# Two transformer blocks on one core: weight blocks at chosen SBUF offsets, and another order in two stages

## The chip, the cores and the metric

One Trainium2 chip, one of its cores. The metric is the device time of one launch in microseconds (us); the kernel before takes 2357.26 us, the median of 3 runs (2355.5 to 2357.8).

## The reference

Two different blocks run one after the other on `x` of 256 tokens by 1024 features, everything in float32; each block has two layers, l = 0 and l = 1.

```python
for l in range(2):                                   # first block
    h = rms(x, ln1[l]) * (1 + sc1) + sh1             # sc, sh, g from silu(c) @ w_mod[l]
    p = h @ w_in[l]                                  # 2756 columns
    # a: top-64 index attention, 4 heads;  b: stick breaking, 4 heads;  c: windowed attention, 8 heads
    x = x + g1 * (rms(concat(a, b, c), g_out[l]) @ w_o[l])
    h = rms(x, ln2[l]) * (1 + sc2) + sh2
    x = x + g2 * ((silu(h @ w_gate[l]) * (h @ w_up[l])) @ w_down[l])     # 2816 inner columns
for l in range(2):                                   # second block, with a context of 256 tokens
    h, hc = norms of x and ctx
    p, pc = h @ w_in_2[l], hc @ w_in_2[l]            # 13328 columns
    # A: mLSTM in both directions, 4 heads;  B: differential attention, 8 heads;  C: a 2-d Fourier mix
    x = x + gate * ((gA*(yA @ w_a_out) + gB*(yB @ w_b_out) + gC*(yC @ w_c_out)) @ w_out)
    ctx = the same for the context, in layer 0 only
```

## The kernel before

All float32 products that matter are made of three float32r matmuls: each operand is split into a part `hi` (rounded to float32r) and the rest `lo`, and hi·hi + hi·lo + lo·hi is summed in PSUM (`mm3`). The weights come from HBM in blocks of 128·kch rows by n columns (mostly 1024 by 256) into `raw` (2 buffers, issued on SP); ACT copies `raw` to `whi`, DVE (or POOL) subtracts into `wlo` (`split_half`, line 381, in two halves of a block). `whi` and `wlo` have two buffers each in the pool `w`, and `take` (line 417) hands a block to the stage that uses it.

A block is used in one of two ways. `dense_t` gives the transposed product: 128 columns of the weight block are the stationary operand of a matmul and h streams, 256 columns of it (one of x or the context) or 512 (both side by side). `dense_n` (called by `natural` and `natural2`) gives the natural product: h is stationary and 256 columns of weights stream. h is `h2`, hi and lo, 128 partitions by 8 chunks by 512 columns, in a pool on the right side of SBUF; the first block uses the 256 columns on its right half.

In time: conditioning and layer 0's mixing (to 219 us), layer 0's feed-forward `swiglu` (line 1172; gate and up 22 blocks, then down 12 blocks, whose moving operand is `ahi`, `alo` in the pool `pm`), layer 1's mixing (435 to 600) and feed-forward (to 807). Then the second block: in layer 0 heads A and pairs B (to 1100), Fourier branch C, gates and merges (1273 to 1713), output projection; in layer 1 the same (heads and pairs from 1795, C from 2001, gates and merges from 2112). In layer 0 x and the context run together, so `dense_t` streams 512 columns; layer 1 needs x alone in most products, 256 columns.

The order of the work is made when the program is built. A planner, the class `Clock`, keeps an estimated time of each engine. Dense blocks follow a fixed list, and the small steps between them (rope, statistics, scores, softmax, top-k, transposes) are items of a `Pipe`: at each tick the items whose inputs the planner holds for ready go one step on, in the order of their ranks. `prm` (line 210) gives the constants of a phase: 0 and 1 are the mixings of the two layers; 2 and 3, and 4 and 5, the two halves of the second block's layers 0 and 1. `RANK` orders the kinds of items of a mixing (sc cr ct cc ir it is sa ar at aa sb bo fc fa fb: `is` is index scores and top-k, `sa` the statistics and `at` the transposes of branch A, `ct` the transposes of branch C, `aa` its attends, `fb` the finish of A and B together). `SEQ` is the order of heads (a) and pairs (b); a third head or pair is begun when the first is drained. `BEHIND` holds items back when the planned DVE or ACT is more than so many us behind PE, `AHD` says how far ahead a raw load is issued, and `DY2` lists the small steps that may go to DVE or POOL, whichever is planned to be done earlier: `t` a copy of keys (`twice`), `s` the rsqrt chains of A and B, `o` those of `finish`.

Every engine has its own queue in that order, and waits only by semaphores; PE executes the matmuls as they were planned. SP's queue holds loads alone (`raw`, and `gw` for the small products `ps_g`). POOL's holds its small chains and the stores and loads of y.

Of the kernel before, what the change touches and what calls it, by code (L numbers as in the profile page):

```python
# [7 lines left out]
F32 = mybir.dt.float32  # L8
F32R = mybir.dt.float32r
# [12 lines left out]
KC = D // 128  # L22
WB = 256
# [5 lines left out]
QA, KA, VA, QI, KI, WI, QB, VB = 0, 256, 320, 384, 640, 704, 708, 1220  # L29

AQ, AK, AV, AG, AO, AZ, BQ, BK, BV, BZ, CU, CZ, MG = (0, 512, 1024, 2048, 2064, 3088, 4112, 5136, 6160, 7184, 8208,
                                                      9232, 10256)
# [169 lines left out]
        return self.clock.used.get(ring[-bufs], 0.0) if len(ring) >= bufs else 0.0  # L202


# [1 line left out]
DEF = dict(BEHIND=6.0, STARTS=2, SPL=2, AHD=1.0, SLACK=0.3, SPW=0.3, PB=0.5, DY2="x", TK=4, DYN=0, Y="", EVERY=2, SPOOL="",  # L206
           RANK="2 2 2 3 0 0 0 2 2 2 1 4 4 1 1 4", ENG="vvvpvpp", ORDER="IBCAV", SPN="0,0", ATT=3, SEQ="aababab", ADA="", ADS="")


def prm(ph):  # L210

    g = {'ADA_0': os.environ.get('ADA0','00 01'), 'ADS_0': os.environ.get('ADS0',''), 'ADA_1': os.environ.get('ADA1','10 11'), 'ADS_1': os.environ.get('ADS1',''), 'BEHIND_4': '1e9', 'BEHIND_5': '1e9', 'BEHIND_0': '8.0', 'BEHIND_1': '8.0', 'BEHIND_2': '1e9', 'BEHIND_3': '1e9', 'SPL_5': '2', 'SPL_4': '1', 'SPL_1': '3', 'SPL_0': '2', 'SPL_3': '2', 'SPL_2': '1', 'ATT_1': '2', 'ATT_0': '3', 'SLACK_2': '-1', 'SLACK_3': '0.3', 'SLACK_0': '0.3', 'SLACK_1': '0.3', 'SLACK_4': '-1', 'SLACK_5': '0.3', 'PB_0': '0.5', 'PB_1': '0.5', 'RANK_0': '0 2 2 3 0 4 0 4 4 1 1 4 4 0 0 3', 'RANK_1': '2 2 2 3 0 4 0 4 2 5 4 1 4 0 2 0', 'DYN_5': '1', 'DYN_4': '1', 'DYN_3': '1', 'DYN_2': '1', 'DYN_1': '1', 'DYN_0': '0', 'ORDER_0': 'IBCAV', 'ORDER_1': 'ICVAB', 'SPOOL_1': '1', 'SPOOL_0': 'x', 'Y_1': 'b', 'Y_0': 'ab', 'ENG_0': 'vpvppvv', 'ENG_1': 'vppvvpp', 'EVERY_1': '2', 'EVERY_0': '2', 'STARTS_5': '1', 'STARTS_4': '1', 'STARTS_3': '1', 'STARTS_2': '1', 'STARTS_1': '2', 'STARTS_0': '2', 'DY2_1': 'x', 'DY2_0': 'x', 'TK_1': '1', 'TK_0': '8', 'AHD_3': '4', 'AHD_2': '4', 'AHD_1': '2.0', 'AHD_0': '1.0', 'AHD_5': '4', 'AHD_4': '4', 'SPN_1': '0,0', 'SPN_0': '0,0'}.get
    p = types.SimpleNamespace(**{k: type(v)(g(f"{k}_{ph}", g(k, v))) for k, v in DEF.items()})
    p.ADA, p.ADS = [[tuple(int(i) for i in u) for u in s.split()] for s in (p.ADA, p.ADS)]
    return p
# [88 lines left out]
class Program:  # L304
# [21 lines left out]
    def phase(self, ph):  # L326
        p = self.p = prm(ph)
        if self.clock:
            self.clock.slow = ph in "01"
        self.pipe.starts, self.pipe.slack, self.pipe.most = p.STARTS, p.SLACK, p.BEHIND  # L330
# [40 lines left out]
    def fetch_g(self, j, now):  # L371
# [6 lines left out]
        self.gblk[j] = t  # L378
        return True

    def split_half(self, now=True):


        j = self.ns
        if j >= self.nd or (j >= 2 and j - 2 not in self.consumed):
            return False
        if not now and self.clock.ready([self.blk[j][0]]) > self.clock.t["pe"] + 1:
            return False
        raw = self.blk[j][0]
        kch, pieces = self.order[j]  # L390
        n = sum(p[4] for p in pieces)
        if self.half == 0:
            for i, nm in ((1, "whi"), (2, "wlo")):
                t = self.wp.tile([128, KC * WB], F32R, name=f"{nm}{j % 2}")
                self.blk[j][i] = t[:, :kch * n].rearrange("p (k c) -> p k c", k=kch)
        k0, k1 = ((0, (kch + 1) // 2), ((kch + 1) // 2, kch))[self.half]
        hi, lo = self.blk[j][1], self.blk[j][2]
        if k1 > k0:
            self.nc.scalar.copy(hi[:, k0:k1], raw[:, k0:k1])
            e = self.nc.gpsimd if str(self.half) in self.p.SPOOL and self.every else self.nc.vector  # L400
            e.tensor_tensor(lo[:, k0:k1], raw[:, k0:k1], hi[:, k0:k1].bitcast(F32), op=ALU.subtract)
        self.half += 1
        if self.half == 2:
            self.half = 0
            self.ns += 1
        return True
# [765 lines left out]
    def swiglu(self, l, h, begin):  # L1172
        nc, pm = self.nc, self.pm
        mod = self.mod[l]
        ahi = pm.tile([128, FC, L], F32R, name="ahi")
        alo = pm.tile([128, FC, L], F32R, name="alo")
        for f in range(FC):
            W = self.take([("w_gate", l, 0, 128 * f, 128), ("w_up", l, 0, 128 * f, 128)])
            ps = self.any_ps().rearrange("p (b t) -> p b t", b=2)
            for j in range(2):  # L1180
                self.dense_t(ps[:, j], W, 128 * j, h, 0, L)
            self.drop()
            th = pm.tile([128, L], F32, name="th", bufs=2)
            nc.scalar.activation(out=th, in_=ps[:, 0], func=AF.Tanh, scale=0.5)
            nc.vector.scalar_tensor_tensor(th, th, 1.0, ps[:, 0], op0=ALU.add, op1=ALU.mult)
            u = pm.tile([128, L], F32, name="mu", bufs=2)
            nc.vector.scalar_tensor_tensor(u, th, 0.5, ps[:, 1], op0=ALU.mult, op1=ALU.mult)
            self.split(u, ahi[:, f], alo[:, f])
            self.fill()
        norm = begin()  # L1190
        for b in range(4):
            pss = [self.any_ps()[:, :L] for j in range(2)]
            for k0 in range(0, FC, 8):
                kc = min(8, FC - k0)
                W = self.take([("w_down", l, 128 * k0, 256 * b, 256)], kc)
                for j in range(2):
                    self.dense_t(pss[j], W, 128 * j, (ahi, alo), 0, L, kch=kc, k0=k0, start=k0 == 0,
                                 stop=k0 + kc == FC)
                self.drop()
                self.fill()  # L1200
            for j in range(2):
                c = 2 * b + j
                nc.vector.scalar_tensor_tensor(self.x[:, c], pss[j], mod[:, 40 + c:41 + c], self.x[:, c],
                                               op0=ALU.mult, op1=ALU.add)
                self.norm_chunk(norm, self.x, c)
        return norm
# [642 lines left out]
    def run(self):  # L1849
# [51 lines left out]
        for l in range(DEPTH):  # L1901
            mod = self.mod[l]
            A = self.gain(mod[:, 8:16], self.ln[:, l, 0:8], f"A1_{l}") if l == 0 else None
            gate, scale = self.mod_gemv(l, 1), self.mod_gemv(l, 2)
            self.pending += [gate, scale] + [self.ada_gemv(*g) for g in prm(str(l)).ADA]
            if l:
                self.drain([ctx_ready])
# [21 lines left out]
            if upto == f"a{l}":  # L1929
                break  # L1930
            self.pending += [self.ada_gemv(*g) for g in prm(str(l)).ADS] + ([] if l else [self.mod_gemv(1, 0)])
            self.norm_rstd(n)
            if l == 0:
# [140 lines left out]
```

## Time and profile before

| what | value |
|---|---|
| median of 3 runs | 2357.26 us |
| lowest, highest | 2355.5, 2357.8 us |
| the profiled execution | 2364.57 us |
| its span, first to last instruction | 2362.8 us |
| its mean granted clock of TensorE | 0.969 |

The profile is of one execution. Busy times are of engines: PE is TensorE's matmuls, PEld its weight loads (beside PE), DVE VectorE, ACT ScalarE, POOL GpSimd. An end of a matmul is modelled, so the distance of starts tells more than the durations. The clock of TensorE has two levels, 2.4 GHz (1.00) and 1.2 GHz (0.50). Every instruction of this kernel goes through one helper, so all have line L170, and groups are told apart by the tiles: `ps_mm<-h,whi` streams h against stationary weights, `ps_mm<-whi,h` streams weights against stationary h.

### The profile page before, as it was taken

To read this page: it belongs to the slowest core of one execution; us is meant where nothing else is said; L and a number is where in the kernel's file an instruction comes from. 1 tells how busy PE (TensorE), PEld (TensorE's weight loads), DVE (VectorE), ACT (ScalarE), POOL (GpSimd) and SP (SyncE) were. 2 spreads that over 40 slices of the span, in tenths; PEclk is the share of its full clock that TensorE was granted. 3 is DMA by queue.
4 is the path that set the end of the run, shared out by engine and by line. 5 is a ranking of instruction groups with operands and counts; after the bars stand their busy time and mean duration, and the time that the engine had idled before them with its cause. 6 is when DMAs were issued, how large, how long until landed. Compare 5 with 4: busy or idle time off the path is not lost. (4 is left out here: it accounts for less than half of the span.)

```text
span 2362.8 us, 39015 instructions
## 1 busy us (share of the span) xinstructions
PE 2247.8 (95%) x15672; PEld 1974.9 (84%) x15672; DVE 1287.4 (54%) x2547; ACT 1032.1 (44%) x1994; POOL 371.7 (16%) x897
## 2 busy tenths in 40 slices
PE   7989999998899999997989999999999999989999
PEld 3756899876899988887878888888898897989999
DVE  3735556575556546666554424335364656655665
ACT  3543445445444444554543323223254445444543
POOL 3311001551000103122022000000020333220000
PEclk8978999998999999998999999999999999999999
DMA  9646985655686522122114434434343232337865
GB/s 331 230 159 220 288 252 181 212 188 196 197 243 187 173 89 72 56 82 72 61 65 139 128 91 113 119 94 114 96 131 90 81 99 74 106 114 201 211 172 170
DMA packets 395061, 348.52 MB, mean 148 GB/s; under 512 B 12768, under 2 KB 364384, under 8 KB 394368
## 3 DMA queue, kind: packets, MB, share of 16 engines
q1 hardware_dynamic: 386752, 321.29, 45.1%
q0 software_dynamic: 6688, 21.66, 2.9%
q10 hardware_dynamic: 1440, 3.08, 0.4%
q8 instruction: 123, 2.02, 0.4%
q14 instruction: 58, 0.48, 0.1%
HBM read 335.50 MB, written 10.49 MB: 146 GB/s over the span
## 5 line engine op out<-in xcount | busy, mean ns | idle before, releaser
L170 DVE TENSOR_TENSOR wlo<-raw,whi 128x1024 fp32r<-128x1024 f32 (+1 forms) x465 | 547.6, 1210 | 449.1 <-ACT whi L170 447.8
L170 ACT CAST whi<-raw 128x1024 fp32r<-128x1024 f32 (+3 forms) x476 | 471.5, 1031 | 216.1 <-PE ps_t L170 63.3
L170 PE MATMUL ps_mm<-whi,h 128*128 128x256 f32 x2752 | 533.9, 291 | 16.1 <-ACT whi L170 6.2
L170 PEld LDWEIGHTS ps_mm<-whi,h 128*128 128x128 f32 x2752 | 440.6, 194 | 48.7 <-issue 19.3
L170 PE MATMUL ps_mm<-wlo,h 128*128 128x256 f32 x1376 | 391.1, 284 | 7.5 <-DVE wlo L170 7.3
L170 PE MATMUL ps_mm<-h,whi 128*128 128x256 f32 (+2 forms) x1656 | 375.5, 321 | 1.9 <-DVE xT L170 1.8
L170 PEld LDWEIGHTS ps_mm<-h,whi 128*128 128x128 f32 (+1 forms) x1656 | 269.2, 187 | 46.9 <-issue 9.0
L170 PEld LDWEIGHTS ps_mm<-wlo,h 128*128 128x128 f32 x1376 | 266.8, 194 | 12.6 <-DVE wlo L170 8.4
L170 PE MATMUL ps_mm<-h,wlo 128*128 128x256 f32 (+2 forms) x828 | 263.0, 318 | 1.1 <-POOL wlo L170 1.1
L170 PE MATMUL ps_s<-h,whi 128*128 128x256 f32 (+1 forms) x1120 | 240.2, 310 | 0.0
L170 PE MATMUL ps_t<-h,whi 128*128 128x256 f32 (+1 forms) x1096 | 234.9, 310 | 2.1 <-ACT h L170 1.5
L170 PEld LDWEIGHTS ps_s<-h,whi 128*128 128x128 f32 x1120 | 181.3, 188 | 18.3 <-ACT th L170 5.6
L170 PEld LDWEIGHTS ps_t<-h,whi 128*128 128x128 f32 x1096 | 179.0, 190 | 19.8 <-ACT th L170 6.3
L170 PE MATMUL ps_s<-h,wlo 128*128 128x256 f32 (+1 forms) x560 | 173.4, 310 | 0.1
L170 PE MATMUL ps_t<-h,wlo 128*128 128x256 f32 (+1 forms) x548 | 169.5, 309 | 0.0
L170 PEld LDWEIGHTS ps_mm<-h,wlo 128*128 128x128 f32 (+1 forms) x828 | 155.1, 187 | 14.7 <-POOL wlo L170 1.3
L170 PE MATMUL ps_g<-gw,c 128*32 128x512 f32 (+1 forms) x640 | 100.8, 640 | 18.0 <-DMA gw<-in_w_mod_dram 8.7
L170 PEld LDWEIGHTS ps_s<-h,wlo 128*128 128x128 f32 x560 | 105.2, 188 | 7.0 <-DVE wlo L170 0.3
L170 PEld LDWEIGHTS ps_t<-h,wlo 128*128 128x128 f32 x548 | 104.2, 190 | 6.2 <-DVE wlo L170 0.2
L170 ACT ACTIVATE M<-ps_s,nmB,rsB 128x512 f32<-128x512 f32 (+1 forms) x96 | 67.0, 702 | 94.2 <-DVE nmB L170 94.2
L170 DVE SCALAR_TENSOR_TENSOR y<-th,y 128x512 f32<-128x512 f32 (+1 forms) x64 | 35.6, 556 | 81.2 <-ACT th L170 67.9
L170 POOL TENSOR_TENSOR sqa<-sqa,sq 128x256 f32<-128x256 f32 x30 | 22.1, 736 | 346.9 <-ACT sq L170 191.3
(406 smaller groups left out, 3726.8 us busy)
## 6 DMA issues: line engine op xcount, KB each, us to landing
raw<-in_w_in_dram SPq DMA_DIRECT2D x72, 1024.0 KB, 5.3
raw<-in_w_in_dram SPq DMA_DIRECT2D x100, 512.0 KB, 4.1
gw<-in_w_mod_dram SPq DMA_DIRECT2D x96, 512.0 KB, 5.3
gw<-in_w_ada_dram SPq DMA_DIRECT2D x64, 384.0 KB, 5.0
raw<-in_w_gate_dram SPq DMA_DIRECT2D x44, 512.0 KB, 4.1
raw<-in_w_up_dram SPq DMA_DIRECT2D x44, 512.0 KB, 5.6
raw<-in_w_down_dram SPq DMA_DIRECT2D x16, 1024.0 KB, 5.1
raw<-in_w_out_dram SPq DMA_DIRECT2D x12, 1024.0 KB, 5.2
```

The lines of the kernel that those rows point to most:

```text
L170: return real(*a, **k)
```

## The change

The blocks of weights get 128 more columns of room, and start at an offset of 0, 16 or 32 elements (0, 64 or 128 bytes), which `place` chooses from the first piece of the block: 0 for those that stream (`natural`, `natural2`, DFT), 16 for those that stand against 512 columns in the second block's layer 0 and for the gate columns AG, 32 for all others. A tile `apart`, which nothing writes or reads, stands behind `ahi` and `alo`; as the pool ends at a fixed address it moves them by 320 bytes in layer 0 and 416 in layer 1. The constants of `prm` change for the phases 0, 1 and 4.

```diff
 def prm(ph):
...
-     'RANK_1': '2 2 2 3 0 4 0 4 2 5 4 1 4 0 2 0'   'AHD_1': '2.0'   'DY2_0': 'x'
-     'BEHIND_4': '1e9'   'SLACK_4': '-1'   'AHD_4': '4'
+     'RANK_1': '2 2 0 3 0 4 5 0 2 1 4 1 4 0 2 2'   'AHD_1': '4.0'   'DY2_0': 't'
+     'BEHIND_4': '5.0'   'SLACK_4': '-1.0'   'AHD_4': '0.5'   'PB_4': '0.5'   'DY2_4': 'sto'   'SEQ_4': 'abaabab'
...
+    @staticmethod
+    def place(pieces):
+        name, l, r, c, w = pieces[0]
+        if name == "dft" or name == "w_in" and not QB <= c < VB:
+            return 0
+        if name == "w_in_2" and (AV <= c < AG or BQ <= c < BZ or CU <= c < CZ):
+            return 0
+        if name == "w_in_2" and (l == 0 or c in (AG,)):
+            return 16
+        return 32
...
-                t = self.wp.tile([128, KC * WB], F32R, name=f"{nm}{j % 2}")
-                self.blk[j][i] = t[:, :kch * n].rearrange("p (k c) -> p k c", k=kch)
+                t = self.wp.tile([128, KC * WB + 128], F32R, name=f"{nm}{j % 2}")
+                o = self.place(pieces)
+                self.blk[j][i] = t[:, o:o + kch * n].rearrange("p (k c) -> p k c", k=kch)
...
         ahi = pm.tile([128, FC, L], F32R, name="ahi")
         alo = pm.tile([128, FC, L], F32R, name="alo")
+        pm.tile([128, 104 if l else 80], F32, name="apart")
```

`SEQ_4` was the default aababab and `DY2_4` the default, which lets nothing choose. The diff also takes the environment variables out of `prm`, whose defaults stay.

## Rows read from the trace of the kernel before

**Rows 1.** The page's first part: busy us (share of the span) xinstructions

```profile
PE 2247.8 (95%) x15672; PEld 1974.9 (84%) x15672; DVE 1287.4 (54%) x2547; ACT 1032.1 (44%) x1994; POOL 371.7 (16%) x897
```

**Rows 2.** Windows: length, PE PEld DVE ACT POOL, PEclk, DMA share, GB/s

```profile
219.00:435.00 216.00, 213.51 (x1754) 196.51 (x1754) 125.73 (x199) 103.57 (x168) 14.58 (x16) 0.98 0.77 236
435.00:565.00 130.00, 115.61 (x816) 90.96 (x816) 79.89 (x221) 65.46 (x147) 65.58 (x104) 0.91 0.62 210
1400.00:1500.00 100.00, 100.00 (x439) 82.05 (x438) 43.94 (x51) 32.92 (x44) 4.29 (x8) 1.00 0.43 114
1795.00:2001.00 206.00, 203.40 (x1465) 181.54 (x1464) 123.73 (x280) 102.19 (x215) 59.33 (x182) 0.99 0.28 87
2112.00:2363.00 251.00, 247.26 (x2115) 246.67 (x2114) 153.92 (x223) 113.54 (x172) 13.96 (x27) 1.00 0.69 188
```

**Rows 3.** Windows of dense stretches, weights stationary, 256 columns

```profile
54.60:59.80 5.20, 5.20 (x47) 5.20 (x45) 2.36 (x2) 1.27 (x2) 4.28 (x14) 1.00 1.03 367
195.40:198.10 2.70, 2.70 (x26) 2.57 (x25) 0.48 (x1) 0.01 (x1) 0.00 (x0) 1.00 0.62 187
708.00:745.00 37.00, 37.00 (x329) 37.00 (x328) 25.09 (x35) 18.48 (x27) 0.00 (x0) 1.00 0.70 199
746.00:807.00 61.00, 61.00 (x518) 61.00 (x517) 30.04 (x35) 27.17 (x37) 4.86 (x7) 1.00 0.62 194
2160.00:2290.00 130.00, 130.00 (x1106) 130.00 (x1105) 81.20 (x116) 60.85 (x92) 4.29 (x8) 1.00 0.71 190
2303.00:2353.00 50.00, 50.00 (x444) 50.00 (x443) 34.46 (x50) 22.93 (x33) 0.00 (x0) 1.00 0.68 195
```

**Rows 4.** Windows of dense stretches, weights moving

```profile
48.40:53.20 4.80, 4.80 (x44) 4.75 (x42) 3.40 (x5) 2.30 (x4) 4.80 (x9) 1.00 1.00 358
2058.00:2062.80 4.80, 4.80 (x43) 4.80 (x42) 3.14 (x4) 2.58 (x4) 4.06 (x10) 1.00 0.00 0
2080.60:2083.00 2.40, 2.40 (x23) 2.40 (x22) 1.01 (x3) 1.32 (x3) 0.19 (x1) 1.00 0.00 0
```

**Rows 5.** Timeline of PE after a start, weights moving: start us, us, instruction

```profile
2027.20 0.28 PE L170 MATMUL ps_mm<-wlo,h 128*128 128x256 f32 x1
...
2027.56 0.28 PE L170 MATMUL ps_mm<-wlo,h 128*128 128x256 f32 x1
...
2028.02 0.39 PE L170 MATMUL ps_mm<-whi,h 128*128 128x256 f32 x2
...
2028.36 0.39 PE L170 MATMUL ps_mm<-whi,h 128*128 128x256 f32 x2
```

**Rows 6.** Timeline of PE: 512 columns, twice, and the DFT's 256

```profile
837.62 0.63 PE L170 MATMUL ps_mm<-h,whi 128*16 128x512 f32 x2
...
841.80 0.39 PE L170 MATMUL ps_mm<-h,whi 128*16 128x512 f32 x1
...
1272.64 0.88 PE L170 MATMUL ps_t<-pq,dft 128*128 128x256 f32 x6
1273.35 0.39 PE L170 MATMUL ps_mm<-h,whi 128*128 128x512 f32 x1
...
1804.34 0.63 PE L170 MATMUL ps_mm<-h,whi 128*128 128x512 f32 x2
...
1808.54 0.63 PE L170 MATMUL ps_mm<-h,whi 128*128 128x512 f32 x2
```

**Rows 7.** Groups by line of DVE, 434 to 606: xcount | busy, mean

```profile
L170 DVE MATCH_REPLACE8 idx_w<-m,idx_w 128x256 f32<-128x256 f32 (+1 forms) x16 | 5.3, 340 | 0.0
...
L170 DVE MAX8 m<-idx_w 128x8 f32<-128x256 f32 (+1 forms) x16 | 4.9, 346 | 0.0
```

**Rows 8.** Timeline of DVE: the mask's last write and its first reader

```profile
522.07 0.32 DVE L170 TENSOR_TENSOR madd<-madd,masks 128x128 f32<-128x128 f32 x1
...
544.47 0.48 DVE L170 CUSTOM_DVE_ANT_0 S<-ps_s,madd,rs 128x256 f32<-128x256 f32 x1
```

**Rows 9.** PE's waits, 435 to 606: us in total, times, longest

```profile
PE ps_t L170 <- ACT S L170: 3.8, 2, 2.5
```

More of the change, by code (lines that the diff above doesn't have):

```diff
@@ L202, in free @@
         return self.clock.used.get(ring[-bufs], 0.0) if len(ring) >= bufs else 0.0
-import os, types
+import types
 DEF = dict(BEHIND=6.0, STARTS=2, SPL=2, AHD=1.0, SLACK=0.3, SPW=0.3, PB=0.5, DY2="x", TK=4, DYN=0, Y="", EVERY=2, SPOOL="",
@@ L210, in prm @@
 def prm(ph):
-    g = {'ADA_0': os.environ.get('ADA0','00 01'), 'ADS_0': os.environ.get('ADS0',''), 'ADA_1': os.environ.get('ADA1','10 11'), 'ADS_1': os.environ.get('ADS1',''), 'BEHIND_4': '1e9', 'BEHIND_5': '1e9', 'BEHIND_0': '8.0', 'BEHIND_1': '8.0', 'BEHIND_2': '1e9', 'BEHIND_3': '1e9', 'SPL_5': '2', 'SPL_4': '1', 'SPL_1': '3', 'SPL_0': '2', 'SPL_3': '2', 'SPL_2': '1', 'ATT_1': '2', 'ATT_0': '3', 'SLACK_2': '-1', 'SLACK_3': '0.3', 'SLACK_0': '0.3', 'SLACK_1': '0.3', 'SLACK_4': '-1', 'SLACK_5': '0.3', 'PB_0': '0.5', 'PB_1': '0.5', 'RANK_0': '0 2 2 3 0 4 0 4 4 1 1 4 4 0 0 3', 'RANK_1': '2 2 2 3 0 4 0 4 2 5 4 1 4 0 2 0', 'DYN_5': '1', 'DYN_4': '1', 'DYN_3': '1', 'DYN_2': '1', 'DYN_1': '1', 'DYN_0': '0', 'ORDER_0': 'IBCAV', 'ORDER_1': 'ICVAB', 'SPOOL_1': '1', 'SPOOL_0': 'x', 'Y_1': 'b', 'Y_0': 'ab', 'ENG_0': 'vpvppvv', 'ENG_1': 'vppvvpp', 'EVERY_1': '2', 'EVERY_0': '2', 'STARTS_5': '1', 'STARTS_4': '1', 'STARTS_3': '1', 'STARTS_2': '1', 'STARTS_1': '2', 'STARTS_0': '2', 'DY2_1': 'x', 'DY2_0': 'x', 'TK_1': '1', 'TK_0': '8', 'AHD_3': '4', 'AHD_2': '4', 'AHD_1': '2.0', 'AHD_0': '1.0', 'AHD_5': '4', 'AHD_4': '4', 'SPN_1': '0,0', 'SPN_0': '0,0'}.get
+    g = {'ADA_0': '00 01', 'ADS_0': '', 'ADA_1': '10 11', 'ADS_1': '', 'BEHIND_4': '5.0', 'BEHIND_5': '1e9', 'BEHIND_0': '8.0', 'BEHIND_1': '8.0', 'BEHIND_2': '1e9', 'BEHIND_3': '1e9', 'SPL_5': '2', 'SPL_4': '1', 'SPL_1': '3', 'SPL_0': '2', 'SPL_3': '2', 'SPL_2': '1', 'ATT_1': '2', 'ATT_0': '3', 'SLACK_2': '-1', 'SLACK_3': '0.3', 'SLACK_0': '0.3', 'SLACK_1': '0.3', 'SLACK_4': '-1.0', 'SLACK_5': '0.3', 'PB_0': '0.5', 'PB_1': '0.5', 'RANK_0': '0 2 2 3 0 4 0 4 4 1 1 4 4 0 0 3', 'RANK_1': '2 2 0 3 0 4 5 0 2 1 4 1 4 0 2 2', 'DYN_5': '1', 'DYN_4': '1', 'DYN_3': '1', 'DYN_2': '1', 'DYN_1': '1', 'DYN_0': '0', 'ORDER_0': 'IBCAV', 'ORDER_1': 'ICVAB', 'SPOOL_1': '1', 'SPOOL_0': 'x', 'Y_1': 'b', 'Y_0': 'ab', 'ENG_0': 'vpvppvv', 'ENG_1': 'vppvvpp', 'EVERY_1': '2', 'EVERY_0': '2', 'STARTS_5': '1', 'STARTS_4': '1', 'STARTS_3': '1', 'STARTS_2': '1', 'STARTS_1': '2', 'STARTS_0': '2', 'DY2_1': 'x', 'DY2_0': 't', 'TK_1': '1', 'TK_0': '8', 'AHD_3': '4', 'AHD_2': '4', 'AHD_1': '4.0', 'AHD_0': '1.0', 'AHD_5': '4', 'AHD_4': '0.5', 'SPN_1': '0,0', 'SPN_0': '0,0', 'PB_4': '0.5', 'DY2_4': 'sto', 'SEQ_4': 'abaabab'}.get
     p = types.SimpleNamespace(**{k: type(v)(g(f"{k}_{ph}", g(k, v))) for k, v in DEF.items()})
```

## The prediction

> **What bounds the kernel now.** I read the page first: TensorE (PE) is busy for 95% of the span, every other engine for 54% or less [rows 1]. Then the busy time stage by stage, for the question where PE waits at all. In the feed-forward of layer 0 (219 to 435 us) it is idle for 2.5 us of 216, in the gates and merges of layer 0's second block not at all (1400 to 1500), in layer 1's merges and output for 3.7 of 251 [rows 2]. There the end is set by how closely matmuls follow each other. DMA reaches a share of 0.77 in the fullest of these stages and VectorE (DVE) 126 of 216 us, so a somewhat faster PE has both behind it. Only the mixing of layer 1 (435 to 565 us) shows slack: PE idle 14.4 us of 130, mean granted clock 0.91, that is 23 us at the 1.2 GHz level [rows 2].
>
> So the number to read is the spacing of matmuls in dense stretches. A window's count holds about 2.4 matmuls that began before it (a record is 0.28 us long), so the spacing is the window over count less 2.4. With the weight block as stationary operand and 256 columns streaming, the spacing is 37.0/326.6 = 113.3 ns in the stretch at 708 us and 50.0/441.6 = 113.2 ns at 2303, but 130/1103.6 = 117.8 ns at 2160, with the same tiles at the same addresses [rows 3]. Nothing waits in either. A stretch thus runs at one of two paces, quick (113.3) or slow (117.8), and keeps it until a gap. Of these stretches 6, with 1,036 matmuls, are quick (first and last in [rows 3], at 195.4 and 2303) and 56 slow (first and last at 54.6 and 2160). The down projection, whose moving operand ahi stands at other addresses than h, runs at 61/515.6 = 118.3 ns in layer 1, never quick [rows 3].
>
> With the operands exchanged (weights stream, h is stationary) it is the other way round: 81 of 133 stretches are quick (first and last at 48.4 and 2080.6), 52 slow (one at 2058, 4.8/40.6 = 118.2) [rows 4]. What differs is the start address of the stationary operand less that of the moving one, modulo 256 bytes: in the built program h2 stands at 224 and the weight blocks at 160, so it is 192 with the weights stationary and 64 with the weights moving; for ahi it is 128 (layer 0) and 32 (layer 1). Of 46 stretches at 64 that begin 215 to 230 ns after the matmul before, 34 settle quick; of 44 such at 192, 3. One that settles begins at 2027: three matmuls take 0.36 us first (2027.20 to 2027.56) and 0.34 a few later (2028.02 to 2028.36) [rows 5].
>
> **The places.** The change moves no instruction here: ACT and DVE write the same elements at another offset, which I cost at nothing (PE never waits in [rows 2] at 1400, with ACT and DVE busy 33 and 44 us of 100). Place 32 moves the stationary blocks by 128 bytes, and the pads move ahi to 224, so that every 256-column matmul with stationary weights gets the difference 64. From the loops there are 6,336 of these: 2,112 in gate and up, 1,056 in down, 1,152 in layer 1's merges, 768 in its gates, 576 in the two output projections of the second block, 384 in w_o, 192 in q and k of the first block's stick heads, 96 in layer 1's aqT. Today they cost 5,300 x 4.5 ns + 1,056 x 0.5 ns (ahi, both layers at layer 1's pace) = 24.4 us more than at the quick pace. If three in four are quick, as 34 of 46 suggest, 1,584 x 4.5 = 7.1 us stay: **17.3 us gained**. Ends: all quick, 24.4; none quick, a loss of 4.1 (the quick stretches of today are two long ones, 908 matmuls, and four short).
>
> The 4,128 matmuls with moving weights keep place 0 and their difference of 64: nothing.
>
> The 512-column matmuls of layer 0's second block go to place 16, difference 0; 2,256 with layer 1's 24 for the gates and its 96 of akT, which get place 32 but are priced with them. They run at 100/(439-1.7) = 228.7 ns [rows 2] (a record of 0.39 us spans 1.7 of them). No stretch of the trace has 512 columns at a steady 0. Nearest rows: a stretch of akT in layer 1 at 233.3 ns (18 matmuls from 1804.34 to 1808.54); the gate columns, whose difference walks through 192, 0, 64 and 128 as k advances, at 4.18/18 = 232.2 ns; and 256 columns at 0 in the DFT, 0.71/6 = 118 ns, not quick [rows 6]. That speaks for a loss, up to 2,256 x 4.6 = 10.4 us. On the other side, the quick 256-column pace is 6.6 ns over 256 columns at 2.4 GHz (106.7 ns); the same excess over 512 columns would be 220, a gain of 19.6 us. I take the middle of these ends, 226.6 ns, since no row is nearer to one than to the other: **4.7 us gained**.
>
> A rule speaks against all of this, in sentences the sum does without. The Trainium skill's page "SBUF — State Buffer", section "SBUF: two separate sides", says that TensorE's reads never wait for anyone, and its page "TensorE: Matmul & The Clock Gate", section "Step-by-step: what each phase is for", that loading the next weights takes no SBUF bandwidth from the running matmul. By these an address cannot matter and the places are worth 0 instead of 22 us; the trace sides against them in the 118.3 of ahi and the unequal shares of quick stretches, and with them in that one address shows both paces.
>
> **The order.** Layer 1's mixing: the index scores and the top-k drop from first to last rank, the statistics and transposes of branch A rise. The top-k is 16 MAX8 and 16 MATCH_REPLACE8, 10.2 us of DVE [rows 7]; the mask made from it is done at 522 and its first reader, an attend of A, comes at 544 [rows 8], so 22 us of attends of C and of the stick heads hide the move. If that cover goes, attend A waits, behind it on PE the w_o blocks: up to +10 (the 10.2 us laid bare). What it could free is PE's wait for S, 3.8 us [rows 9], and some of the half-clock time, 23 us which cost 11.7: up to -9. I take **2 us gained**. AHD_1 issues raw loads earlier on SP, where only loads (raw and gw) stand; PE shows no wait for DMA there: nothing. DY2_0 lets two small copies of layer 0 go to DVE: nothing, since PE has other blocks to run beside them; were one laid bare it is some tenths of a us.
>
> Layer 1's second block (1795 to 2001): PE is idle 2.6 us of 206 at clock 0.99 [rows 2], so another order of heads and pairs can gain 3 us at most. The moved steps' DMAs: raw loads on SP in the order of use, and the y stores on POOL, each of which waits for DVE at the queue's head with the rsqrt chains behind it; 's' takes those chains away from there to DVE, busy 124 of 206 us. BEHIND_4 makes the plan hold items back when DVE or ACT runs 5 us behind; PE would then wait at the drains, at most the 5 us. I take nothing, -3 to +5.
>
> **Sum.** 17.3 + 4.7 + 2 = 24 us. The profiled execution took 2364.57 us (span 2362.8 and 1.8 around it): 2340.6 for it. The median of the runs is 7.3 us lower, 2357.26, which gives **2333.3**.
>
> **Rivals.** (B) Both groups settle: all 256-column ones quick and the 512-column ones at 220: 24.4 + 19.6 + 2 = 46 us, 2311. For: the pace once quick is kept through 444 matmuls [rows 3]; against: the DFT at difference 0 [rows 6]. (C) The places do nothing: only how a stretch starts decides. Then 2355 with the order's 2 us, 2357 without; this is also what the skill's rule gives. For: one address, two paces; against: ahi. (D) Slower: place 16 puts the 440 us of 512-column matmuls on 233.3 ns, +10.4 us, while the long 256-column stretches draw the slow pace, +4.1: 2357.3 + 14.5 - 2 = 2370. With a share p quick the 256-column gain is 28.5p - 4.1, so D decides below p = 0.44.
>
> **How the numbers follow.** Forecast 0.46 (own range 2320 to 2346), B 0.22, C 0.15, D 0.17. A measurement of this kernel tells 0.2% (4.7 us) from no change. Faster: forecast, B and 0.04 of C, 0.72; same 0.11; slower 0.17. The range runs from below B to the top of C, 2306 to 2360, and leaves out D and a little of B.
>
> **What would show it.** Right: in the changed trace the windows over the two feed-forwards and layer 1's merges hold about 444 matmuls per 50 us where they are dense, instead of 427; down is no longer at 118.3; a window of 100 us in the merges of layer 0 holds 443 or more instead of 439; the stretches with moving weights are as mixed as now. Wrong: some 430 there (D), the same mix of paces at every difference (C), or a mixing of layer 1 whose PE idle time rises over 20 us. The forecast fails if the share of quick stretches at 64 does not carry over from moving to stationary weights: that is its weakest step.

## The result, and the profile after

The changed kernel takes 2335.07 us, the median of 6 runs (2324.4 to 2344.74), beside 2357.53 for the kernel before: a ratio of 0.9897, 95% interval 0.9866 to 0.9928, so 17 to 32 us less. The forecast was 2333.3, its range 2306 to 2360. The profiled execution is the slowest of the six: 2344.74 us, span 2343.0.

First the page's first part, of the kernel after, as in [rows 1]:

```profile
PE 2228.7 (95%) x15672; PEld 1961.0 (84%) x15672; DVE 1311.5 (56%) x2637; ACT 1031.5 (44%) x1995; POOL 343.5 (15%) x779
```

PE has the same 15,672 instructions and 19.1 us less of busy time; the span fell by 19.8 us. Time went out of matmuls, not out of waits. Where, is read from windows cut at the same matmul in both kernels (first matmul of a stage to the first of the next). The columns are those of [rows 2]. Before; in order gate and up, down, the whole of layer 1's mixing, gate and up, down, the 512-column gates and merges, then from there to layer 1's branch C, and to the end:

```profile
243.15:369.79 126.64, 126.64 (x1064) 116.17 (x1056) 72.81 (x103) 54.45 (x82) 0.00 (x0) 1.00 0.86 261
369.79:434.05 64.26, 64.26 (x545) 64.26 (x544) 38.08 (x61) 37.55 (x64) 11.46 (x12) 1.00 0.57 181
434.05:622.42 188.37, 165.45 (x1198) 135.06 (x1197) 114.99 (x301) 92.12 (x197) 73.55 (x112) 0.91 0.58 192
622.42:745.25 122.83, 122.83 (x1058) 114.48 (x1057) 72.86 (x104) 54.58 (x82) 0.00 (x0) 1.00 0.78 230
745.25:807.73 62.48, 62.48 (x531) 62.48 (x529) 30.56 (x35) 27.80 (x39) 4.86 (x7) 1.00 0.60 189
1273.35:1712.83 439.48, 439.48 (x1923) 360.58 (x1922) 176.83 (x205) 129.18 (x165) 14.65 (x28) 1.00 0.41 112
1712.83:2063.28 350.45, 337.41 (x2505) 308.62 (x2504) 209.99 (x449) 172.74 (x353) 92.09 (x262) 0.98 0.31 95
2063.28:2359.38 296.10, 288.95 (x2422) 283.12 (x2420) 180.44 (x281) 136.89 (x231) 26.06 (x67) 0.99 0.64 176
```

The same stages after:

```profile
235.81:358.16 122.35, 122.35 (x1059) 112.38 (x1057) 72.84 (x103) 54.73 (x82) 0.00 (x0) 1.00 0.87 265
358.16:420.89 62.73, 62.73 (x544) 62.73 (x543) 38.08 (x61) 37.49 (x63) 11.46 (x12) 1.00 0.58 185
420.89:610.34 189.45, 166.14 (x1198) 131.87 (x1197) 113.27 (x300) 92.07 (x199) 74.39 (x112) 0.91 0.60 198
610.34:730.73 120.39, 120.39 (x1058) 114.38 (x1057) 75.07 (x106) 54.88 (x82) 0.00 (x0) 1.00 0.77 224
730.73:790.57 59.84, 59.84 (x530) 59.84 (x529) 30.58 (x35) 27.60 (x39) 4.87 (x7) 1.00 0.62 197
1257.32:1692.56 435.24, 435.24 (x1923) 360.37 (x1922) 177.07 (x205) 128.97 (x165) 14.67 (x28) 1.00 0.41 113
1692.56:2044.66 352.10, 335.48 (x2509) 306.66 (x2508) 224.43 (x532) 172.84 (x353) 62.49 (x163) 0.98 0.31 95
2044.66:2339.56 294.90, 290.32 (x2418) 284.31 (x2416) 181.31 (x289) 136.19 (x231) 21.42 (x48) 0.98 0.63 176
```

PE is busy through all of the five dense stages in both kernels, at clock 1.00, and each is shorter: 4.3 + 1.5 + 2.4 + 2.6 + 4.2 = 15.1 of the 19.8 us. The mixing of layer 1 is 1.1 us longer, the stages between the fifth and the sixth row together 1.1 us longer, the last two stages together within half a us. Layer 0's mixing, ahead of these rows, was 7.4 us shorter, which the experiments take back: it scatters.

Then the pace, in windows of dense stretches after (as [rows 3], and 100 us of the same stage as the window of [rows 2] at 1400; the first row is from layer 0's down):

```profile
395.00:415.00 20.00, 20.00 (x172) 20.00 (x171) 15.22 (x25) 11.88 (x20) 1.47 (x2) 1.00 0.57 180
678.00:728.00 50.00, 50.00 (x443) 50.00 (x442) 33.09 (x46) 25.24 (x38) 0.00 (x0) 1.00 0.70 196
735.00:785.00 50.00, 50.00 (x443) 50.00 (x443) 25.13 (x27) 22.85 (x32) 4.87 (x7) 1.00 0.63 199
1300.00:1400.00 100.00, 100.00 (x443) 82.81 (x442) 29.12 (x31) 25.09 (x30) 0.54 (x1) 1.00 0.40 104
2130.00:2260.00 130.00, 130.00 (x1106) 130.00 (x1105) 78.30 (x107) 61.23 (x90) 4.29 (x8) 1.00 0.73 196
2282.00:2332.00 50.00, 50.00 (x443) 50.00 (x442) 35.08 (x50) 24.32 (x35) 0.00 (x0) 1.00 0.68 200
```

Gate and up, layer 1's down, and the end of layer 1's merges are quick, 50/(443 - 2.4) = 113.5 ns; layer 1's down was never quick before. Layer 0's down is quick for its first 230 matmuls only; the other 298 of its 528 run at the slow pace, 20/(172 - 2.4) = 117.9 ns. The 512-column window holds 443 instead of 439: 226.6 ns. But the long stretch of layer 1's merges (1,343 matmuls) is as slow as before, with 1106 in 130 us. Counted over the stretches, 45 of the 58 with stationary weights are quick, and with them 4,056 of 6,195 matmuls.

### The profile page after: what moved, and what is told of

Same layout as the page of the kernel before. It is cut to its first block, busy times and chain, and to the rows that moved or that the text cites. A ratio compares the mean times of both kernels' runs of the same rounds, so it can differ in the third digit from the quotient of the medians.

```text
span 2343.0 us, 38997 instructions
## 1 busy us (share of the span) xinstructions
PE 2228.7 (95%) x15672; PEld 1961.0 (84%) x15672; DVE 1311.5 (56%) x2637; ACT 1031.5 (44%) x1995; POOL 343.5 (15%) x779
```

## Experiments

All ratios are to the kernel before in runs of the same chip, with 95% intervals. Paces are mean distances of starts within a dense stretch; stage lengths are taken as in the windows above. The difference of two start addresses is that of the prediction, and an address is on the 32-byte grid when it is a multiple of 32. Of the one long line of constants in `prm` the diffs show only those that change.

**1. The places alone, and the order alone.** Run e1 is the changed kernel with the constants of before (places and pads alone); run e2 is the kernel before with the changed constants. The edit of e1, that of e2 is its reverse:

```diff
-    'RANK_1': '2 2 0 3 0 4 5 0 2 1 4 1 4 0 2 2'   'AHD_1': '4.0'   'DY2_0': 't'
-    'BEHIND_4': '5.0'   'SLACK_4': '-1.0'   'AHD_4': '0.5'   'PB_4': '0.5'   'DY2_4': 'sto'   'SEQ_4': 'abaabab'
+    'RANK_1': '2 2 2 3 0 4 0 4 2 5 4 1 4 0 2 0'   'AHD_1': '2.0'   'DY2_0': 'x'
+    'BEHIND_4': '1e9'   'SLACK_4': '-1'   'AHD_4': '4'
```

> The places and the pads alone, with the constants of the kernel before, so that the order of the instructions stays the old one. Theory P (the places bring the gain, by the pace of matmuls): 2335 to 2341 us, 256 columns with stationary weights at a mean of some 115.0 ns, 512 columns at 226.7, and single runs that differ by up to 10 us, as the pace is drawn anew at each start. Theory O (the other order brings a good part, as the first mixing is 7.4 us shorter in the changed kernel's profile): 2343 to 2348. Theory N (places do nothing): 2357.

> The constants of the changed kernel alone, weights and ahi at the old places. Theory P: 2355 to 2360 us, since the stages that the order touches add up to little. Theory O: 2346 to 2352 (7.4 us from layer 0's mixing, given back in part by layer 1's). In both the paces stay as before: 229.0 ns for 512 columns, 117.8 for nearly all stretches with 256.

Places: 2341.77 us, 0.9928 (0.9910 to 0.9945), 13 to 21 us less. Order: 2357.13, 0.9988 (0.9977 to 0.9999), 0.2 to 5.4 us less. The gates and merges of layer 0's second block in the two, places first; with them layer 1's merges with the places, and layer 0's gate and up with the order alone:

```profile
1254.88:1690.12 435.24, 435.24 (x1922) 360.37 (x1921) 176.91 (x205) 129.01 (x165) 14.65 (x28) 1.00 0.40 113
2120.00:2250.00 130.00, 130.00 (x1150) 130.00 (x1149) 79.70 (x109) 62.68 (x91) 4.29 (x8) 1.00 0.75 205
```

```profile
236.70:362.93 126.23, 126.23 (x1058) 116.17 (x1057) 72.82 (x103) 54.76 (x82) 0.00 (x0) 1.00 0.84 257
1264.88:1704.34 439.46, 439.46 (x1922) 360.60 (x1921) 177.14 (x205) 129.25 (x165) 14.65 (x28) 1.00 0.40 112
```

With the places the 512-column stage is 435.24 us to the hundredth, with the old ones 439.5, whatever the order. And the long stretch of layer 1's merges came out quick here, 1150 matmuls in 130 us, by the same addresses as above. So the places bring nearly all, theory P, though the time lies just above its 2335 to 2341; the order is a small gain. Theory O falls: layer 0's mixing takes 231.3 us with the old order too (230.3 and 231.0 in two other runs, e4 and e11), so the 237.5 of the profile before was a long draw.

**2. What of an address counts.** Run e3 gives every weight block of the changed kernel another offset, two blocks in a row at each:

```diff
-                o = self.place(pieces)
+                o = 8 * (5 * (j // 2) % 16)
```

Run e4 is the kernel before with its weights where they were and h2 moved by 128 bytes:

```diff
         self.h2 = [p2.tile([128, KC, T2], F32R, name=f"h2{i}") for i in range(2)]
+        p2.tile([128, 32], F32, name="apart2")
```

> The changed kernel with every weight block at another offset, 0 to 480 bytes in steps of 32, two blocks in a row at each: a look at the pace by the difference of the start addresses. Theory P with the difference modulo 256: 256 columns quick (113.3 ns) in most stretches at 64, in both uses; at 192 and the rest 117.8 to 119; 512 columns 226.7 at 0, 229 at 192, 233.2 at 64. In sum some 10 us over the changed kernel, 2340 to 2355. If instead the place of the weights itself decides, the paces follow the offset and not the difference, and differ between ahi and h at one difference.

> The kernel before with h2 and all that stands under it on the right side 128 bytes lower, the weight blocks where they were. Difference: stationary weights against h 64 instead of 192 (5,280 matmuls), moving weights 192 instead of 64, 512 columns 64 instead of 192, down 0 and 160. If the difference decides: stationary 256-column stretches mostly quick, moving ones nearly all slow (117.8), 512 columns at 233.2; in time -10 + 9 + 9.5 us, 2361 to 2370. If the place of the weights decides: all paces as before, 2357.

From the timeline of PE in the sweep, first and last start of four blocks without a gap: 256 columns at 64 (96 matmuls) and at 160 (84), 512 columns at 0 and at 64 (96 each):

```profile
678.83 0.39 PE L170 MATMUL ps_t<-h,whi 128*128 128x256 f32 x2
689.59 0.28 PE L170 MATMUL ps_mm<-h,wlo 128*128 128x256 f32 x1
...
756.42 0.28 PE L170 MATMUL ps_t<-ahi,whi 128*128 128x256 f32 x1
766.38 0.28 PE L170 MATMUL ps_mm<-ahi,wlo 128*128 128x256 f32 x1
...
1400.21 0.62 PE L170 MATMUL ps_mm<-h,whi 128*128 128x512 f32 x2
1421.75 0.40 PE L170 MATMUL ps_mm<-h,wlo 128*128 128x512 f32 x1
...
1444.38 0.63 PE L170 MATMUL ps_t<-h,whi 128*128 128x512 f32 x2
1466.55 0.40 PE L170 MATMUL ps_t<-h,wlo 128*128 128x512 f32 x1
```

10.76/95 = 113.3 ns, 9.96/83 = 120.0, 21.54/95 = 226.7, 22.17/95 = 233.4. All the stretches of the sweep, in ns (where there are several, each occurs):

```
difference    0      32     64           96           128          160    192    224
256, stat.    120.0  118.3  113.3|117.8  117.3|118.7  118.6|120.0  120.0  117.8  116.6
256, moving   120.0  118.4  113.3|117.8  117.1|118.7  118.7        119.9  117.8  116.7|117.9
512, stat.    226.7  233.3  233.3        234.3        232.4        233.4  228.9  233.3
```

The two uses have nearly the same row, and ahi the same as h. At 192 the sweep shows the slow pace alone; the profiles with the old places have quick stretches there too, 6 of 62 in the kernel before. The kernel with h2 moved runs as its differences say (windows: gates and merges at 64; layer 1's merges at 64; down of layer 1 at 160):

```profile
1300.00:1400.00 100.00, 100.00 (x430) 80.71 (x430) 32.38 (x36) 26.89 (x33) 2.15 (x4) 1.00 0.42 112
2155.00:2285.00 130.00, 130.00 (x1150) 130.00 (x1149) 81.31 (x111) 63.10 (x93) 4.29 (x8) 1.00 0.74 201
739.00:799.00 60.00, 60.00 (x502) 60.00 (x501) 28.23 (x33) 26.95 (x37) 4.84 (x7) 1.00 0.60 196
```

100/(430 - 1.7) = 233.5 ns, 130/1147.6 = 113.3, 60/499.6 = 120.1. Of its moving stretches, now at 192, 121 of 132 are slow, where 52 of 133 were; of the stationary ones, now at 64, 46 of 64 are quick, where 6 of 62 were. It took 2366.78 us, the forecast 2361 to 2370. The weights hadn't moved: the pair of addresses counts, not a place. The sweep's time, 2369.02, was missed (2340 to 2355): I had not counted that its mean over the differences is slower than the old places.

**3. Which pace a stretch at 64 draws.** In the eight profiles with this difference on the 32-byte grid (before, after and its repetition, and the runs e1, e2, e4, e10, e11) the distance from the matmul before the gap to the one after it, in the trace's nanoseconds, goes with the pace: after 206 or 207 ns 78 of 78 stretches are quick, after 223 or 224 162 of 165, after 225 to 227 1 of 55, after 200 or 201 68 of 271. Other gaps lie between: after 221 or 222 ns 211 of 244 are quick, after more than 300 ns 104 of 189. So at some lengths the gap settles the pace, and at the commonest, 200 or 201 ns, it stays a draw. What sets the gap to the nanosecond stays open.

**4. Between the steps, and off the 32-byte grid.** Run e5 sweeps offsets in between, in the changed kernel:

```diff
-                o = self.place(pieces)
+                o = [20, 30, 28, 18, 36, 14, 44, 34, 52, 31, 60, 15, 4, 33, 12, 17][j // 2 % 16]
```

It showed moving weights at 144 at 113.4 ns in 9 stretches of 9; run e6 puts the blocks of w_in and w_in_2 that stream there (those of the DFT stay at 0):

```diff
-            return 0
+            return 44
```

Run e7 moves h2, and in the same way ahi, alo, fhi and part, to 240 modulo 256 and sweeps again:

```diff
-        self.h2 = [p2.tile([128, KC, T2], F32R, name=f"h2{i}") for i in range(2)]
+        self.h2 = [p2.tile([128, KC * T2 + 64], F32R, name=f"h2{i}")[:, 4:4 + KC * T2].rearrange("p (k c) -> p k c", k=KC) for i in range(2)]
...
-                o = self.place(pieces)
+                o = 4 * (7 * (j // 2) % 16)
```

> The sweep again, at the differences between the steps of 32 bytes: odd multiples of 16, and 4 and 8 bytes to either side of 64 and of 0 (for stationary weights; for moving ones the negative of it). Theory P1 (the pace hangs on the difference modulo 32 bytes and on its multiple, so that a few bytes are rounded away): 60 to 72 like 64, quick at 113.3 ns; 248 to 8 with 512 columns like 0, 226.7. Theory P2 (each step of 4 bytes counts): only 64 itself is quick, and the rest 116.5 to 120; with 512 columns only 0 itself at 226.7 and the rest 229 to 234. Open, and the reason for the look: whether a difference in between is better than 113.3 or 226.7, or quick without fail. Time 2355 to 2375.

> The changed kernel, with the blocks that stream (weights moving, 4,128 matmuls) at 176 bytes instead of 0, so that the difference is 144 instead of 64; the rest as in the changed kernel. In the fine sweep all 9 stretches of moving weights at 144 ran at 113.4 ns. Theory L (at 144 there is one pace only, while at 64 the gap at the start draws one of two): all of these stretches at 113.4, 1,350 slow matmuls x 4.4 ns = 6 us less than the changed kernel, 2326 to 2332. Theory S (the 9 were chance: 0.65 to the 9th power is 0.02): a third of them slow as before, 2335 to 2341.

> The changed kernel with h2, ahi, fhi and part 16 bytes further (240 modulo 256), and the weight blocks swept in steps of 16 bytes: the operand that is not a weight is now off the 32-byte grid, the weights at every second block. Theory A (beside the difference it counts which operand is off the 32-byte grid: moving off and stationary on at 144 is the lasting quick case): with the weights stationary 144 runs at 113.4 in every stretch, as moving weights at 144 did; with both off, the multiples of 32 repeat the first sweep (64 two-paced, 0 at 120.0, 512 columns at 0 at 226.7). Theory D (the difference alone counts): stationary at 144 stays at 120.0 as in the fine sweep. Time 2360 to 2385.

Fine sweep, 2382.5 us, over the 2355 to 2375 expected: theory P2 in that each step of a few bytes counts, though not in all its numbers (144 with moving weights is quick, stationary weights take 115.6 at 8, and 512 columns came out at 226.7 in one of two stretches at 240). At 60 and 68 stationary weights take 119.5 and 118.3, at 56 and 72 117.8 and 118.2; 512 columns take 232.3 at 4 and 233.3 at 248. Nothing is under 113.3 or 226.7. The slowest pace of all, 123.2, is that of moving weights 4 bytes off.

Moving weights at 144: 133 of 137 stretches settled at 113.4 to 115.5, theory L in the pace, but the time is 2336.5, 0.9882 (0.9862 to 0.9901), not clear of the changed kernel's 0.9897. The stretches are mostly of 24 matmuls and settle slowly: the mean distance over all of them fell from 115.24 to 115.02 only, 0.8 us. The 6 us were reckoned from settled paces.

The second sweep, 2378.68 us, first and last start of: stationary weights against ahi at 144 (84 matmuls), 512 columns at 96, 512 columns at 0 (96 each):

```profile
374.61 0.28 PE L170 MATMUL ps_s<-ahi,whi 128*128 128x256 f32 x1
384.01 0.28 PE L170 MATMUL ps_t<-ahi,wlo 128*128 128x256 f32 x1
...
1298.82 0.61 PE L170 MATMUL ps_s<-h,whi 128*128 128x512 f32 x2
1320.35 0.40 PE L170 MATMUL ps_s<-h,wlo 128*128 128x512 f32 x1
...
1431.09 0.62 PE L170 MATMUL ps_s<-h,whi 128*128 128x512 f32 x2
1453.05 0.40 PE L170 MATMUL ps_s<-h,wlo 128*128 128x512 f32 x1
```

9.40/83 = 113.3, where the fine sweep had 120.0 at 144: theory A there. But its other half falls. With both operands 16 bytes off the grid, 0 gives 118.3 (120.0 on it), 512 columns 231.2 at 0 (226.7) and 226.6 at 96 (234.3), and 64 gives 113.3 in 16 stretches of 16. A common shift of both changes the pace, so the difference alone is a sound rule only on the grid.

**5. A kernel in which every stretch is quick.** Both operands off the grid, 64 in both uses, 512 columns at 32; beside it, as e9, the changed kernel again. Run e8 has h2, ahi, alo, fhi and part as e7, yacc likewise, and in `place` (DFT excepted):

```diff
-            return 0
+            return 4
...
-            return 16
+            return 28
...
-        return 32
+        return 36
```

> The changed kernel with h2, ahi, alo, fhi, yacc and part 16 bytes further than a 256-byte boundary less 32 (240 modulo 256) and the weights at the same differences, 64 in both uses, so that both operands are off the 32-byte grid; 512 columns at 32, which the second sweep showed at 226.7. Theory A (off the grid 64 has one lasting pace, as in its 4 and 12 stretches of the second sweep): all 256-column stretches quick, means of dense spacing 113.5 (stationary) and 114.4 (moving) against 114.0 to 115.0 and 115.0 to 115.4, so 6 to 11 us under the changed kernel, 2325 to 2330, and a narrower spread of runs. Theory S (the few stretches of the sweep were chance, or owe their pace to the block before): the mix of paces of the changed kernel, 2334 to 2341.

> The changed kernel once more, unaltered, on the same chip as the run beside it. All theories: 2335 to 2342 us, a ratio of 0.987 to 0.993, and another draw of paces: the stretch of 1,343 matmuls in layer 1's merges quick or slow (6 us), 512 columns at 226.7 again.

```profile
2125.00:2255.00 130.00, 130.00 (x1150) 130.00 (x1149) 82.88 (x118) 62.08 (x93) 4.30 (x8) 1.00 0.76 203
355.00:385.00 30.00, 30.00 (x267) 30.00 (x266) 16.03 (x30) 19.54 (x33) 6.17 (x6) 1.00 0.61 193
389.00:415.00 26.00, 26.00 (x232) 26.00 (x231) 17.77 (x27) 14.28 (x23) 3.17 (x3) 1.00 0.62 196
```

All 199 stretches of 256 columns are quick (136 moving, 63 stationary; rows of layer 1's merges and layer 0's down), mean distances 114.33 and 113.55. That is theory A for the pace; the time, 2334.44 us, is not in its 2325 to 2330. The changed kernel again had 44 of 59 stationary stretches quick and its long one slow, mean 115.23. By these means e8 was to gain more on it than the 6 to 11 us expected ((115.23 - 113.55) x 6,150 + (115.20 - 114.33) x 3,700 ns = 13.5 us against this execution). The medians are 2334.44 and 2335.68 us, ratios 0.9868 (0.9841 to 0.9895) and 0.9886 (0.9858 to 0.9915): 4 us, not told from nothing, nor from 13. And with no pace left to draw the runs still went from 2325.71 to 2338.7, so that the spread of the changed kernel isn't that of the paces alone, as I had expected. In the profiles it is layer 0's mixing that moves most: with the new constants 221.7 us in e9, at clock 0.95, 225.8 in e8, at 0.90, 232.5 in e6, at 0.88, and 236.4 in e7, at 0.87. That its clock makes the spread isn't shown.

**6. The order's parts.** Run e10 is the kernel before with DY2_0 alone:

```diff
-    'DY2_0': 'x'
+    'DY2_0': 't'
```

Run e11 is e2 with the reverse of this edit (the other constants alone), and e12 is e8 with it.

> The kernel before with DY2_0 't' alone: in layer 0's mixing two small copies may go to DVE. In the profiles so far that stage took 230 to 238 us with the old order (3 of them) and 222 to 233 with the new one (6). Theory M (the order's gain sits in this stage, the step costed at nothing): 3 to 5 us under the kernel before, ratio 0.998. Theory C (the stage only scatters, with the clock granted there): no difference, within 2 us.

> The kernel before with the changed kernel's constants except DY2_0: layer 1's mixing order and the order of layer 1's second block. Theory M: within 1 us of the kernel before. Theory of the prediction (2 us from layer 1's mixing, nothing from the second block): 2 us less, which 5 rounds can hardly tell from nothing.

> The off-grid places of the run e8_offgrid with DY2_0 left at 'x', as the candidate that could beat both kernels. Theory M2 (with layer 1's new order DY2_0 is worth nothing or costs 0.1%, since it then no longer moves the plan of layer 1's mixing): a ratio of 0.985 to 0.988, all 256-column stretches quick. Theory C2 (the two go together in layer 0's mixing): 0.988 to 0.991.

DY2_0 alone is slower: 2368.99 us, 1.0040 (1.0018 to 1.0062), 4 to 15 us. Neither theory had that. The rest alone is 0.9976 (0.9963 to 0.9988), 3 to 9 us faster, more than either theory had; both together, run e2, 0.9988. The windows of layer 1's mixing with DY2_0 alone, and the 25 us in it at the lowest clock:

```profile
423.52:620.62 197.10, 170.79 (x1198) 138.64 (x1198) 117.26 (x303) 91.86 (x196) 73.47 (x112) 0.88 0.54 180
525.00:550.00 25.00, 21.64 (x104) 13.34 (x96) 9.66 (x32) 17.02 (x41) 5.18 (x5) 0.66 0.56 189
```

Before, the 25 us at the same distance from the start of the stage, 101.5 us (the stage is the third row of the first table):

```profile
535.53:560.53 25.00, 21.96 (x117) 13.98 (x114) 14.03 (x46) 16.34 (x37) 5.18 (x5) 0.73 0.73 247
```

In these two executions layer 1's mixing is 8.7 us longer with a constant of layer 0's: 197.1 against 188.4, 5.3 us of it PE's busy time, at clock 0.88 against 0.91, in that window 0.66 against 0.73. In the other two profiles with the old order the stage takes 187.1 (e1) and 190.9 us (e4). Its matmuls stand in another order there, 64 of 1,196 moved, as the planner's clock runs on from stage to stage; with the new ranks DY2_0 moves none of them, and costs nothing that can be told (e2 at 0.9988, e11 at 0.9976). Ahead of layer 0's down it moves 92 of 2,388 matmuls with either ranks. That the moved order, and not something else of the constant, makes the loss is the likeliest reading and no run of its own.

A rival stands untested: another draw of paces. In run e11's profile the long stretch of layer 1's merges, 1,295 matmuls here, came out quick, though at the old difference of 192:

```profile
2140.00:2270.00 130.00, 130.00 (x1149) 130.00 (x1149) 82.11 (x113) 63.27 (x93) 4.30 (x8) 1.00 0.73 201
```

130/(1149 - 2.4) = 113.4 ns. In e10's and e2's profiles it was slow, as before. All matmuls with stationary weights and 256 columns took 761.9 us in e11, 767.9 before, 770.6 in e2 and 772.9 in e10, so these draws alone make differences of the size that the two runs show; whether they did so in the other executions isn't on record.

Run e12 took 2331.28 us (2328.79 to 2334.05), 0.9868 (0.9843 to 0.9894), theory M2. It is the lowest median of all; its interval overlaps with the changed kernel's.

## Why the prediction was right, step by step

- **The bound and the view.** Right. The spacing of matmuls sets the end: 15.1 of the 19.8 us came out of five stages in which PE never stopped, and no other stage grew by more than 1.7.
- **256 columns, -17.3 us.** Right in mechanism, somewhat too large. Three in four were taken as quick. By stretches it was 45 of 58, 47 of 67 and 44 of 59 (after, e1, after again), by matmuls 65, 78 and 59%, since the one stretch of 1,343 was slow twice. All matmuls with stationary weights and 256 columns, gaps included, took 767.9 us before and 754.2, 752.3 and 759.0 after: 9 to 16 us gained. The time before is itself a draw: the three other profiles with the old places have 761.9 to 772.9. The share did carry over from one use to the other, the step called weakest; run e4 exchanges the two uses and the shares go with the difference. What the argument missed is that a gap of 223 and one of 226 ns are two cases, which it counted together.
- **ahi.** Right in layer 1: down runs at 113.3 ns (59.84 us/528) instead of 118.3. In layer 0 298 of the 528 matmuls are slow at the difference 64 as well, in after, e1 and e9 alike. So of the signs named ahead, 444 matmuls per 50 us and the end of down's slow pace, neither holds in every stage.
- **512 columns, -4.7 us.** The number was right, 226.7 ns against 226.6 and 4.2 us less in the sum of these matmuls; its reason, the middle of two ends, was none, so this term came out by luck. At 64 it would have been 233.3, the loss of the rival D.
- **Moving weights, nothing.** Right: 115.42 ns before, 115.24 after.
- **The order, -2 us.** The sum was right (0.2 to 5.4 us), its parts were not. The step that failed is "DY2_0 lets two small copies of layer 0 go to DVE: nothing, since PE has other blocks to run beside them". With the old ranks the constant costs 4 to 15 us, and it moves the plan of a later stage; that this makes the loss is argued, not shown. The new ranks and the rest gain 3 to 9 without it. Where these lie isn't shown either: layer 1's mixing is 188.1 us in that run against 188.4, the stages of layer 1's second block scatter as much, and the quick long stretch of its profile alone is worth 1,295 x 4.4 ns = 5.8 us. So the 2 us came out in part by luck: neither what DY2_0 does nor where the gain lies is as the prediction had it.
- **The rivals.** B (all quick, 512 columns at 220): off the grid all 256-column stretches are quick, but 220 occurs at no difference of three sweeps. C (the places do nothing) falls by run e1. It was also how the prediction read the rule of the Trainium skill (page "SBUF — State Buffer", section "SBUF: two separate sides": TensorE's reads never wait for anyone). The runs do not agree with that reading: the same instruction takes 113.3 or 120.0 ns by its operands' addresses. Whether the longer pace is a wait at SBUF isn't shown. D needed 233.3 at place 16 and under 44% quick, and had neither.
- **The sum.** 24 us forecast; 22.5 by the medians, 24.3 by the ratio. The places, 22.0 in the sum, measured 13 to 21 alone.

## What to carry to other kernels

Where TensorE never stops, divide the columns by the distance of starts and compare stretches of one shape: two paces at one clock can point to the operands' addresses. Then sweep the offset of one operand block by block within one run, for each width and use apart, and mind that a start address 4 or 16 bytes off can change the answer. And where a planner carries its clock through the program, try each constant by itself: it can move the order of another stage.

## What the runs showed of the hardware that I had not expected

- The pace of a dense stretch hangs on the pair of start addresses of the stationary and the moving operand, from 113.3 to 123.2 ns for 256 columns and from 226.7 to 234.3 for 512 (up to 234.7 off the grid), all at granted clock 1.00.
- At the difference 64 on the 32-byte grid two paces are possible, and at some lengths the gap ahead goes with which: after 223 or 224 ns 162 of 165 stretches are quick, after 225 to 227 1 of 55. After 200 or 201 ns both occur. At 192 both occur too, the quick one seldom.
- 16 bytes off the grid one pair had one pace only, 113.3, in all 199 stretches of run e8.
- 226.7 ns, within 0.1, was the least for 512 columns at all differences tried.
